# Modulation vectors moved among the mLSTM heads, the second half's operand built in pieces, and a GEMM's first weights fetched an iteration earlier

## The chip, the cores and the metric

The kernel runs on one core of one Trainium2 chip. The metric is the device time of one execution in microseconds (us). Engines are named as in the profile: PE is TensorE, which multiplies matrices; PEld its weight loads; DVE is VectorE, ACT ScalarE, POOL GpSimd, SP SyncE, which here only issues transfers (DMAs).

## The reference, cut to what matters

Two transformer blocks run one after the other on one sequence of 1024 positions with 1024 channels, all in float32. The first has three attention branches and an MLP; the second a mixer (a two-direction mLSTM with four heads beside a pooling branch) and another MLP. In the second block the normalised inputs and the updates are scaled and shifted by six modulation vectors that come from one conditioning vector `c`:

```python
def second_block(x, c, w_ada, b_ada, ...):
    c_act = jax.nn.silu(c)
    mod = c_act @ w_ada[l] + b_ada[l]          # 6 x 1024 numbers
    sh1, sc1, gt1, sh2, sc2, gt2 = jnp.split(mod, 6, axis=-1)
    h = _modulate(_rmsnorm(x, g_mix[l]), sh1, sc1)       # h * (1 + scale) + shift
    x = x + gt1[:, None, :] * _mixer(h, ...)
    h = _modulate(_rmsnorm(x, g_ffn[l]), sh2, sc2)
    a = jnp.square(jax.nn.relu(jnp.einsum('bsd,df->bsf', h, w_ff1[l])))
    x = x + gt2[:, None, :] * jnp.einsum('bsf,fd->bsd', a, w_ff2[l])
    return _rmsnorm(x, g_final)
```

Each MLP is `relu(h @ w1)**2 @ w2` with 1024 x 4096 and 4096 x 1024 weights. So `sh1` and `sc1` are wanted when the first MLP has ended and the mixer's input is normalised; the other four (`gt1`, `sh2`, `sc2`, `gt2`) not before the mixer's output.

## The kernel before, in words

Every float32 operand is split into a high and a low part of a faster format, and a product of two operands is three matmuls: high x high, low x high, high x low. For weights, `parts_of` (L1246) makes the high part `wh` by an ACT copy (L1249) and the remainder `wl` by a DVE subtraction (L1250). `product` (L1253) is a block of 128 x 512 results: four slices of the contraction, so twelve matmuls.

**One MLP** (`mlp`, L1233, called for both blocks) multiplies by a scheme with seven products for a 2 x 2 split of the matrices instead of eight. Its operand is normalised in two halves. The helper `make_t` (L1105) builds the second half's: a first piece at once, and `rest` (L1128), which forms the operands that the tables `TQ["t2"]`, `["t3"]`, `["t4"]` hold. `rest` works in four PSUM banks, four channel blocks at a time; six banks (`mm_bank`) are all that products and `rest` have. The **first GEMM** starts with products that need only the first half (`first_of`, L1313): blocks 4, 5, 6 and 0, then `rest`, then blocks 1, 2 and 3. Then 16 iterations follow (`for m in range(NM)`), each with weight sums on POOL (`sums`, L1306), five to seven products, and results written to DRAM. The **second GEMM** runs over four quarters `ch` of the hidden layer. A quarter loads blocks of the weights `a11`, `a21`, `a22`, `a12`, POOL forms their sums (`s_`, L1462, and further sums at L1483, L1484), and seven groups of products follow, each with an operand that `second` (L1393) reads back from DRAM and splits. In `ch` 0 the order is `a11`, `s_`, `a11` again (now a difference), and so on.

**The modulation vectors** come from the generator `ada` (L1152). There are twelve groups of 512 columns. For a group DVE takes eight weight tiles of 128 x 512 (`adaw`, two buffers, 256 KB a transfer on SP's queue), multiplies the first by a scalar for each partition (L1180) and adds seven more (fused multiply-add, L1182) into `ada`; PE transposes the sum in four pieces (L1189), and DVE adds them up into `mod`. `tick` after a DVE instruction takes one step of the generator, and puts what it issues behind that instruction. In the kernel before, ticks stand so close together in the first MLP that all twelve groups end in it.

**The heads.** `mlstm` (L1877) goes over eight chunks in two directions for each head. A step makes two PE products into a PSUM bank, DVE updates the state `C` (L1898) and computes the denominator `den` (L1902 to L1904), and ACT or DVE writes the head's rows. Between steps PE works on other products (`fill2`, `steps`).

What order the instructions of each engine have is fixed when the program is built, by a scheduler that follows the code's data and its issue order. Each engine runs its own list in that order, and waits for others by semaphores.

Of the kernel before, what the change touches and what calls it, by code (L numbers as in the profile page):

```python
# [60 lines left out]
def block_kernel(ctx, tc, x, mem, positions, g_mix, w_in, b_gate, sinks, g_mem, w_mem_kv, w_proj_swa, w_proj_dsa,  # L61
# [1090 lines left out]
    def ada(modp):  # L1152
# [80 lines left out]
    def mlp(PB, xt, d, w1, w2, scale, post, begin, middle, tick=lambda ins: None, gains=None, each=lambda i, e: None,  # L1233
# [66 lines left out]

        e1s, e2s, sas = {}, {}, {}
# [20 lines left out]
        rest_t.pop()()  # L1322
        begin[2]()
        first_of(1)
        first_of(2)
        first_of(3)
        e1s[0] = w_of(wep, 0, "we", 2)
        sums(0)
        for m in range(NM):
# [15 lines left out]
            tick(V.tensor_tensor(q12, p5, u2, op=OP.add))  # L1345
# [3 lines left out]
            tick(V.tensor_tensor(q12, a, q12, op=OP.add))  # L1349
# [10 lines left out]
            tick(V.tensor_tensor(q22, p5, u3, op=OP.add))  # L1360
# [26 lines left out]
        braw = hA([P, DC, 512], F32, tag="h_lo")  # L1387
        nb = [0]

        def second(n, ch):  # L1390
            i = nb[0]
            nb[0] += 1
            r = braw[:, 4 * (i % 2):4 * (i % 2) + 4]  # L1393
            nc.sync.dma_start(r, d[n][:, 4 * ch:4 * ch + 4, :])
            j = 1 if i == 27 else i % 3
            t_ = ((hA, "h_hi"), (PB, "h_hi"), (PB, "h_lo"))[j]
# [728 lines left out]
```

## Time and profile before

| what | us |
|---|---|
| median of 3 runs | 2686.01 (2683.36 to 2688.73) |
| the profiled execution | 2684.82 |
| its span in the trace | 2683.1 |
| PE busy | 2522.5 |
| DVE busy | 1905.7 |
| ACT busy | 1198.5 |
| POOL busy | 985.1 |

The span is the stretch from the first to the last instruction in the trace; the profiled execution has 1.7 us beside it. The first MLP runs from about 880 to 1600 us, the heads from 1684 to 1910, the second MLP from about 1990 to the end. "Idle before" in a row is the time in which the engine had nothing to run ahead of that instruction, with the arrow to the instruction on another engine that released it. PEclk is the granted clock of TensorE: 1.00 is 2.4 GHz and 0.50 is 1.2 GHz.

### The profile page before, as it was taken

To read this page: it belongs to the slowest core of one execution; us is meant where nothing else is said; L and a number is where in the kernel's file an instruction comes from. 1 tells how busy PE (TensorE), PEld (TensorE's weight loads), DVE (VectorE), ACT (ScalarE), POOL (GpSimd) and SP (SyncE) were. 2 spreads that over 40 slices of the span, in tenths; PEclk is the share of its full clock that TensorE was granted. 3 is DMA by queue.
4 is the path that set the end of the run, shared out by engine and by line. 5 is a ranking of instruction groups with operands and counts; after the bars stand their busy time and mean duration, and the time that the engine had idled before them with its cause. 6 is when DMAs were issued, how large, how long until landed. Compare 5 with 4: busy or idle time off the path is not lost. (4 is left out here: it accounts for less than half of the span.)

```text
span 2683.1 us, 34924 instructions
## 1 busy us (share of the span) xinstructions
PE 2522.5 (94%) x12560; PEld 2108.3 (79%) x12560; DVE 1905.7 (71%) x3208; ACT 1198.5 (45%) x2218; POOL 985.1 (37%) x727
## 2 busy tenths in 40 slices
PE   7999999999999888997999969999998999999997
PEld 6899987788878677786777856888786788778886
DVE  7685868844455667877999996655557455698898
ACT  6575764434334534444433332332435455534333
POOL 3001123431002344445565651111433444576554
PEclk9999999999999899998999989999998999999999
DMA  3121023221155366658754312322452544654431
GB/s 115 52 57 47 25 64 102 83 71 32 60 178 171 103 223 212 192 184 293 246 199 153 110 32 62 125 80 63 143 162 92 194 160 161 244 203 152 170 110 63
DMA packets 284257, 348.02 MB, mean 130 GB/s; under 512 B 14364, under 2 KB 191284, under 8 KB 276916
## 3 DMA queue, kind: packets, MB, share of 16 engines
q1 hardware_dynamic: 242404, 259.95, 30.4%
q10 hardware_dynamic: 40720, 82.70, 8.5%
q0 software_dynamic: 960, 3.15, 0.3%
q8 instruction: 99, 1.62, 0.2%
q14 instruction: 74, 0.61, 0.1%
HBM read 256.54 MB, written 89.19 MB: 129 GB/s over the span
## 5 line engine op out<-in xcount | busy, mean ns | idle before, releaser
L1255 PE MATMUL mm<-h_hi,wh 128*128 128x512 f32 (+1 forms) x1136 | 456.3, 402 | 33.6 <-DVE q L1120 10.3
L1257 PE MATMUL mm<-h_hi,wl 128*128 128x512 f32 (+1 forms) x1136 | 452.0, 399 | 22.8 <-DVE wl L1250 22.8
L1256 PE MATMUL mm<-h_lo,wh 128*128 128x512 f32 (+1 forms) x816 | 321.6, 394 | 0.0
L1255 PEld LDWEIGHTS mm<-h_hi,wh 128*128 128x128 f32 x1136 | 221.9, 195 | 82.8 <-ACT wh L1249 13.0
L1257 PEld LDWEIGHTS mm<-h_hi,wl 128*128 128x128 f32 x1136 | 221.4, 195 | 75.3 <-DVE wl L1250 29.6
L1249 ACT CAST wh<-q 128x1024 fp32r<-128x1024 f32 x116 | 122.0, 1053 | 345.3 <-PE mm L1256 294.3
L1256 PE MATMUL mm<-h_hi,wh 128*128 128x512 f32 (+1 forms) x624 | 246.1, 395 | 0.0
L1250 DVE TENSOR_TENSOR wl<-q,wh 128x1024 fp32r<-128x1024 f32 x116 | 192.2, 1659 | 22.4 <-ACT wh L1249 21.0
L1256 PEld LDWEIGHTS mm<-h_lo,wh 128*128 128x128 f32 x816 | 157.8, 193 | 31.4
L1401 POOL TENSOR_TENSOR h_hi<-h_lo,h_hi 128x512 fp32r<-128x512 f32 x76 | 126.2, 1679 | 127.8 <-ACT h_hi L1400 127.6
L133 ACT CAST wh<-wr 128x1024 fp32r<-128x1024 f32 (+5 forms) x107 | 97.2, 911 | 151.6 <-PE mm L418 47.1
L1255 PE MATMUL mm<-q,wh 128*128 128x512 f32 x384 | 150.1, 391 | 0.0
L1256 PE MATMUL mm<-q,wh 128*128 128x512 f32 x384 | 149.7, 390 | 0.0
L1257 PE MATMUL mm<-q,wl 128*128 128x512 f32 x384 | 149.6, 390 | 0.0
L1256 PEld LDWEIGHTS mm<-h_hi,wh 128*128 128x128 f32 x624 | 121.7, 195 | 24.1
L134 POOL TENSOR_TENSOR wl<-wr,wh 128x1024 fp32r<-128x1024 f32 (+5 forms) x40 | 78.3, 1964 | 160.6 <-ACT wh L133 159.1
L1641 PE MATMUL mm<-h_hi,wh 128*128 128x512 f32 x320 | 131.6, 411 | 0.9 <-DVE kn L1674 0.8
L1643 PE MATMUL mm<-h_hi,wl 128*128 128x512 f32 x320 | 126.5, 395 | 0.0
L1642 PE MATMUL mm<-h_lo,wh 128*128 128x512 f32 x320 | 125.4, 392 | 0.8 <-DVE h_lo L1081 0.8
L1250 DVE TENSOR_TENSOR wl<-we,wh 128x1024 fp32r<-128x1024 f32 x50 | 79.1, 1582 | 59.8 <-ACT wh L1249 55.9
L1255 PE MATMUL mm<-h_lo,wh 128*128 128x512 f32 (+1 forms) x304 | 115.4, 380 | 0.6 <-ACT wh L1249 0.6
L598 ACT ACTIVATE sbit<-sbit 128x1024 bf16<-128x1024 bf16 (+2 forms) x99 | 93.6, 947 | 50.0 <-DVE sbit L597 48.1
(594 smaller groups left out, 6991.2 us busy)
## 6 DMA issues: line engine op xcount, KB each, us to landing
h_lo<-ml_t SPq DMA_DIRECT2D x32, 1024.0 KB
adaw<-in_w_ada_dram SPq DMA_DIRECT2D x96, 256.0 KB
h_lo<-ml_q SPq DMA_DIRECT2D x24, 1024.0 KB
wr<-in_w_in_dram SPq DMA_DIRECT2D x42, 512.0 KB
wr<-in_w_out_dram SPq DMA_DIRECT2D x32, 512.0 KB
q<-in_w_mlp_out_dram SPq DMA_DIRECT2D x16, 1024.0 KB
q<-in_w_ff_dram SPq DMA_DIRECT2D x16, 1024.0 KB
ml_t<-h_lo ACTq DMA_DIRECT2D x60, 256.0 KB
```

What stands on the lines that cost most here:

```text
L133: A.copy(hi, r)
L134: (eng or V).tensor_tensor(lo, r, raw(hi), op=OP.subtract)
L598: A.activation(b, b, AF.Copy, accum_out=cnt[:, j:j + 1])
L1249: A.copy(hi, r)
L1250: (eng or V).tensor_tensor(lo, r, raw(hi), op=OP.subtract)
L1255: mm(a, wt[0][:, k], b[0][:, k, sl], start=(k == 0), stop=False)
L1256: mm(a, wt[0][:, k], b[1][:, k, sl], start=False, stop=False)
L1257: mm(a, wt[1][:, k], b[0][:, k, sl], start=False, stop=(k == 3))
L1401: (G if c % 2 else V).tensor_tensor(lo[:, c], r[:, c], raw(hi[:, c]), op=OP.subtract)
L1641: mm(a, hi[:, k, :], r_hi, start=(k == 0), stop=False)
L1642: mm(a, hi[:, k, :], r_lo, start=False, stop=False)
L1643: mm(a, lo[:, k, :], r_hi, start=False, stop=(k == DC - 1))
```

## The change

Three edits, of which the second and third act in both MLPs.

1. Ticks in the first MLP become fewer (in the first GEMM three in two iterations instead of eight, in the second a few in each quarter). Four groups of columns, `sh1` and `sc1`, have to be done there, which `while done[0] < 4` makes sure of; a fifth has its DVE instructions there. The others go on in the heads: a tick stands after each step's first `den` operation, and in the forward direction after every second row update. What would be left is finished behind the last head, where the second normalisation's gain (`gain_of(1, ...)`) is computed. The pool with the `adaw` buffers stays open until then.
2. `rest` becomes a generator. It takes two banks for two channel blocks, forms `t2` and `t4` in them, and hands over; between its pieces stand the first products of blocks 1, 2 and 3.
3. In the last iteration of the first GEMM the operand of the second one's first group (`second("q12", 0)`, now `b_1`) and its first weights (`w_1`) are fetched. The weights come as two pieces of 256 columns into tiles `we` and `wr` of the first GEMM, and are split into parts right behind the loop. The whole block `a11` is still loaded for POOL's sums.

```diff
         def rest():
-            b = [mm_bank() for _ in range(4)]
             t2, t3, t4 = (TQ[n] for n in ("t2", "t3", "t4"))
-            for c in range(4):
-                norm(4 + c, b[c])
-            for c in range(4):
-                V.tensor_tensor(src(c), b[c], src(c), op=OP.subtract)
-                A.copy(src(4 + c), b[c])
-                V.tensor_tensor(b[c], b[c], t1[c], op=OP.subtract)
-                split_to(t2[0][:, c, :], t2[1][:, c, :], b[c])
+            for cs in ((0, 1), (2, 3)):
+                b = {c: mm_bank() for c in cs}
+                for c in cs:
+                    norm(4 + c, b[c])
+                for c in cs:
+                    V.tensor_tensor(src(c), b[c], src(c), op=OP.subtract)
+                    A.copy(src(4 + c), b[c])
+                    V.tensor_tensor(b[c], b[c], t1[c], op=OP.subtract)
+                    split_to(t2[0][:, c, :], t2[1][:, c, :], b[c])
+                for c in cs:
+                    z = first(4 + c, t1[c])
+                    V.tensor_tensor(b[c], z, b[c], op=OP.subtract)
+                    split_to(t4[0][:, c, :], t4[1][:, c, :], b[c])
+                yield
             for c in range(4):
                 split_to(hi1[:, 4 + c, :], lo1[:, 4 + c, :], src(4 + c))
+            yield
             for c in range(4):
                 split_to(t3[0][:, c, :], t3[1][:, c, :], src(c))
-            for c in range(4):
-                z = first(4 + c, t1[c])
-                V.tensor_tensor(b[c], z, b[c], op=OP.subtract)
-                split_to(t4[0][:, c, :], t4[1][:, c, :], b[c])
+            yield
...
         first_of(0)
-        rest_t.pop()()
+        more = rest_t.pop()()
+        next(more)
+        first_of(1)
+        next(more)
+        first_of(2)
+        next(more)
+        first_of(3)
+        next(more)
         begin[2]()
-        first_of(1)
-        first_of(2)
-        first_of(3)
...
         for m in range(NM):
             u2, q11, u3, q12 = s1s[m % 4], q11s[m % 4], u3s[m % 2], q12s[m % 2]
+            if m == NM - 1:
+                b_1 = second("q12", 0)
+                w_1 = []
+                for u in range(2):
+                    w_1.append(wep([P, 4, 256], F32, tag="we", bufs=2) if u else wp([P, 4, 256], F32, tag="wr", bufs=2))
+                    nc.sync.dma_start(w_1[u], quarter_of(0, 0, 0, u * 256, 256))
...
-            tick(V.tensor_tensor(q12, p5, u2, op=OP.add))
+            r = V.tensor_tensor(q12, p5, u2, op=OP.add)
+            if m % 2:
+                tick(r)
...
         save_later()
+        w_1 = [parts_of(r) for r in w_1]
         wep.close()
...
-            if not late_ and e % 4 != 1 and (hf or e < 4):
+            if not late_ and e == 2 and not (hf and ch_[0] == 3):
                 tick(r)
...
-            b = second("q12", ch)
+            b = second("q12", ch) if ch else b_1
...
-            for e, wt in blocks(a11):
+            for e, wt in blocks(a11, None if ch else w_1):
...
         if hf == 0:
-            for _ in ada_:
-                pass
...
+            while done[0] < 4:
+                next(ada_)
+            gain_of(0, "g_mix_2")
...
                 den = wk_([P, 1], tag="den", bufs=3)
-                V.tensor_scalar(den, nm[:, P:P + 1], -1.0, flo[:, r0 + c:r0 + c + 1], op0=OP.mult, op1=OP.max)
+                tick1(V.tensor_scalar(den, nm[:, P:P + 1], -1.0, flo[:, r0 + c:r0 + c + 1], op0=OP.mult, op1=OP.max))
...
-                    V.scalar_tensor_tensor(hm(c), nm[:, :P], den, hm(c), op0=OP.mult, op1=OP.add)
+                    r = V.scalar_tensor_tensor(hm(c), nm[:, :P], den, hm(c), op0=OP.mult, op1=OP.add)
+                    if i % 2:
+                        tick1(r)
...
     pool_out(3)
+    for _ in ada_:
+        pass
+    gain_of(1, "g_ffn_2")
```

The first place is DVE's list at the start of the first MLP, where `rest` and the first products meet. L1295 (L1301 after) evicts a first product, L1110 to L1144 (to L1141 after) and L1120 belong to `rest`, `wl` at L1250 (L1256) is a weight remainder. Before:

```order
L1120 TENSOR_TENSOR h_lo_1869_9100<-h_lo_1737_8334,h_hi_1868_9099 128x512 x2
L1120 TENSOR_TENSOR q_1875_9114<-mm_1911_9314,q_1874_9113 128x512
L1120 TENSOR_TENSOR q_1877_9116<-h_lo_1737_8334,q_1876_9115 128x512 x4
L1144 TENSOR_TENSOR mm_1908_9311<-t512_1894_9213,mm_1908_9311 128x512
L1144 TENSOR_TENSOR mm_1909_9312<-t512_1895_9215,mm_1909_9312 128x512
L1144 TENSOR_TENSOR mm_1910_9313<-t512_1896_9217,mm_1910_9313 128x512
L1120 TENSOR_TENSOR q_1879_9118<-mm_1908_9311,q_1878_9117 128x512
L1120 TENSOR_TENSOR q_1879_9118<-mm_1909_9312,q_1878_9117 128x512
L1120 TENSOR_TENSOR q_1879_9118<-mm_1910_9313,q_1878_9117 128x512
L1144 TENSOR_TENSOR mm_1911_9314<-t512_1897_9219,mm_1911_9314 128x512
L1295 TENSOR_TENSOR h_hi_1736_8333<-mm_1916_9392,h_hi_1736_8333 128x512
```

After:

```order
L1137 TENSOR_TENSOR mm_1908_9311<-mm_1908_9311,t512_1894_9213 128x512
L1137 TENSOR_TENSOR mm_1909_9312<-mm_1909_9312,t512_1895_9215 128x512
L1110 SCALAR_TENSOR_TENSOR mm_1916_9370<-h_lo_1737_8334,cols_4_75,tp_1893_9208 128x512
L1120 TENSOR_TENSOR q_1875_9114<-mm_1908_9311,q_1874_9113 128x512
L1120 TENSOR_TENSOR q_1875_9114<-mm_1909_9312,q_1874_9113 128x512
L1141 TENSOR_TENSOR mm_1908_9311<-t512_1894_9213,mm_1908_9311 128x512
L1141 TENSOR_TENSOR mm_1909_9312<-t512_1895_9215,mm_1909_9312 128x512
L1301 TENSOR_TENSOR h_hi_1736_8333<-mm_1914_9353,h_hi_1736_8333 128x512
L1120 TENSOR_TENSOR q_1879_9118<-mm_1908_9311,q_1878_9117 128x512
L1120 TENSOR_TENSOR q_1879_9118<-mm_1909_9312,q_1878_9117 128x512
L1135 TENSOR_TENSOR h_lo_1737_8334<-mm_1915_9369,h_lo_1737_8334 128x512
```

Before, the eviction in the last row comes when `rest` is all but done; after, one stands in the midst of it, and `t4` (`q_1879`) of the first two blocks is formed ahead of the later two blocks' `t2`.

The second place is DVE's list in the first GEMM of the first MLP, over about one iteration. `ada<-adaw` is the modulation. Before:

```order
L1349 TENSOR_TENSOR h_lo_1737_8334<-mm_1999_9911,h_lo_1737_8334 128x512
L1182 SCALAR_TENSOR_TENSOR ada_1980_9799<-adaw_1989_9854,silu_1832_8844,ada_1980_9799 128x512
L1359 TENSOR_TENSOR h_lo_1737_8334<-mm_2005_9943,h_hi_1736_8333 128x512
L1360 TENSOR_TENSOR h_lo_1737_8334<-mm_1993_9868,h_lo_1737_8334 128x512
L1182 SCALAR_TENSOR_TENSOR ada_1980_9799<-adaw_1996_9905,silu_1832_8844,ada_1980_9799 128x512
L1250 TENSOR_TENSOR wl_2017_10033<-we_1994_9881,wh_2016_10032 128x1024
L1365 TENSOR_TENSOR h_lo_1737_8334<-mm_2007_9964,h_lo_1737_8334 128x512
L1182 SCALAR_TENSOR_TENSOR ada_1980_9799<-adaw_2000_9926,silu_1832_8844,ada_1980_9799 128x512
```

After:

```order
L1400 TENSOR_TENSOR h_lo_1737_8334<-mm_2011_10027,h_hi_1736_8333 128x512
L1401 TENSOR_TENSOR h_lo_1737_8334<-mm_2001_9958,h_lo_1737_8334 128x512
L1256 TENSOR_TENSOR wl_2022_10114<-we_2002_9971,wh_2021_10113 128x1024
L1406 TENSOR_TENSOR h_lo_1737_8334<-mm_2012_10045,h_lo_1737_8334 128x512
L1186 SCALAR_TENSOR_TENSOR ada_1946_9592<-adaw_1987_9876,silu_1832_8844,ada_1946_9592 128x512
L1256 TENSOR_TENSOR wl_2025_10136<-wr_2009_10020,wh_2024_10135 128x512
L1410 TENSOR_TENSOR h_lo_1737_8334<-mm_2014_10063,h_hi_1736_8333 128x512
L1411 TENSOR_TENSOR h_lo_1737_8334<-mm_2014_10063,h_lo_1737_8334 128x512
```

Of three modulation instructions in such a stretch one is left.

The third place is DVE's list at the beginning of head 0. Before:

```order
L1903 TENSOR_TENSOR den_2741_14854<-den_2741_14854,sc_2738_14848 128x1
L1898 SCALAR_TENSOR_TENSOR C_2745_14878<-C_2740_14852,dec_2723_14764,sc_2744_14876 128x129
L1904 RECIPROCAL den_2741_14854<-den_2741_14854 128x1
L1902 TENSOR_SCALAR den_2746_14880<-tp_2743_14873,flo_2721_14754 128x1
L1898 SCALAR_TENSOR_TENSOR C_2751_14902<-C_2745_14878,dec_2723_14764,tp_2750_14900 128x129
L1903 TENSOR_TENSOR den_2746_14880<-den_2746_14880,tp_2743_14873 128x1
L134 TENSOR_TENSOR wl_2787_15071<-wr_2788_15072,wh_2786_15070 128x1024
L1904 RECIPROCAL den_2746_14880<-den_2746_14880 128x1
```

After:

```order
L1929 TENSOR_SCALAR den_2688_14690<-sc_2685_14683,flo_2654_14529 128x1
L1186 SCALAR_TENSOR_TENSOR ada_2681_14664<-adaw_2523_13796,silu_1832_8844,ada_2681_14664 128x512
L1930 TENSOR_TENSOR den_2688_14690<-den_2688_14690,sc_2685_14683 128x1
L1925 SCALAR_TENSOR_TENSOR C_2692_14712<-C_2687_14688,dec_2656_14539,sc_2691_14710 128x129
L1931 RECIPROCAL den_2688_14690<-den_2688_14690 128x1
L1929 TENSOR_SCALAR den_2693_14714<-tp_2690_14707,flo_2654_14529 128x1
L1925 SCALAR_TENSOR_TENSOR C_2698_14738<-C_2692_14712,dec_2656_14539,tp_2697_14736 128x129
L1930 TENSOR_TENSOR den_2693_14714<-den_2693_14714,tp_2690_14707 128x1
L134 TENSOR_TENSOR wl_2733_14889<-wr_2734_14890,wh_2732_14888 128x1024
L1186 SCALAR_TENSOR_TENSOR ada_2681_14664<-adaw_2682_14666,silu_1832_8844,ada_2681_14664 128x512
```

Two multiply-adds now stand among the `den` and `C` instructions of two steps here; in all of head 0 there are thirteen, and two of the tensor-by-scalar form.

## Rows read from the trace of the kernel before

**Rows 1.** The page's head and part 1: busy us of each engine

```profile
span 2683.1 us, 34924 instructions
...
PE 2522.5 (94%) x12560; PEld 2108.3 (79%) x12560; DVE 1905.7 (71%) x3208; ACT 1198.5 (45%) x2218; POOL 985.1 (37%) x727
```

**Rows 2.** TensorE's waits: line, releaser; us in total, times, longest us

```profile
PE tp L1189 <- DVE ada L1182: 25.5, 7, 8.8
PE mm L1257 <- DVE wl L1250: 23.1, 12, 9.7
PE tp L1024 <- DVE q L1009: 20.3, 4, 15.9
PE mm L1255 <- ACT wh L1249: 10.7, 7, 3.8
PE mm L1255 <- DVE q L1120: 10.3, 2, 5.7
...
PE mm L1255 <- ACT x L1292: 6.8, 1, 6.8
...
PE mm L1255 <- ACT h_hi L1292: 6.3, 1, 6.3
```

**Rows 3.** Timeline, TensorE's three first waits for ada: start, us, engine, line

```profile
972.75 1.09 PE L1189 MATMUL tp<-ident,ada 128*128 128x128 f32 x4 [8.77 <-DVE ada L1182]
...
1017.34 0.63 PE L1189 MATMUL tp<-ident,ada 128*128 128x128 f32 x4 [3.48 <-DVE ada L1182]
...
1141.07 0.63 PE L1189 MATMUL tp<-ident,ada 128*128 128x128 f32 x4 [3.55 <-DVE ada L1182]
```

**Rows 4.** The modulation's DVE instructions: duration ns min/median/max, first and last start

```profile
L1182 DVE SCALAR_TENSOR_TENSOR ada<-adaw,silu,ada x84: 731/970/2569, 945.7 to 1444.1; 128x512 f32<-128x512 f32 x84
L1180 DVE TENSOR_SCALAR ada<-adaw,silu x12: 475/478/1402, 943.6 to 1413.0; 128x512 f32<-128x512 f32 x12
```

**Rows 5.** Windows: length, busy PE PEld DVE ACT POOL, granted clock, DMA share, GB/s

```profile
967.61:977.85 10.24, 5.10 (x14) 4.23 (x15) 6.55 (x7) 3.42 (x6) 6.04 (x4) 0.50 0.63 189
1141.69:1145.10 3.41, 3.41 (x10) 2.65 (x9) 2.72 (x3) 2.94 (x5) 1.61 (x2) 0.50 0.55 179
912.99:930.06 17.07, 9.14 (x20) 6.25 (x21) 13.75 (x20) 6.03 (x12) 2.66 (x2) 0.50 0.18 51
2032.56:2049.63 17.07, 8.77 (x19) 5.97 (x20) 14.13 (x20) 7.59 (x13) 1.57 (x1) 0.50 0.24 75
1237.26:1244.09 6.83, 6.18 (x14) 4.40 (x15) 5.82 (x9) 5.96 (x11) 3.80 (x5) 0.50 1.05 410
1257.74:1267.98 10.24, 5.23 (x12) 4.18 (x13) 7.78 (x4) 1.53 (x2) 7.89 (x5) 0.50 0.25 94
1400.00:1450.00 50.00, 45.12 (x196) 36.84 (x195) 50.00 (x58) 15.71 (x23) 25.21 (x13) 0.97 0.57 199
1684.00:1717.00 33.00, 31.59 (x192) 26.57 (x193) 26.51 (x93) 12.14 (x33) 7.03 (x6) 1.00 0.46 148
1717.00:1910.00 193.00, 192.54 (x1010) 161.82 (x1008) 112.00 (x305) 58.31 (x129) 30.20 (x59) 1.00 0.19 58
```

**Rows 6.** Timeline, TensorE's waits at the start of either second GEMM

```profile
1237.87 0.80 PE L1255 MATMUL mm<-h_hi,wh 128*128 128x512 f32 x1 [3.85 <-ACT wh L1249]
...
1262.75 0.80 PE L1257 MATMUL mm<-h_hi,wl 128*128 128x512 f32 x1 [9.71 <-DVE wl L1250]
...
2338.84 0.50 PE L1257 MATMUL mm<-h_hi,wl 128*128 128x512 f32 x1 [2.13 <-DVE wl L1250]
...
2361.97 0.79 PE L1257 MATMUL mm<-h_hi,wl 128*128 128x512 f32 x1 [4.92 <-DVE wl L1250]
```

**Rows 7.** Timeline there in the first MLP: DVE remainders, POOL sums

```profile
1252.28 12.68 DVE L1250 TENSOR_TENSOR wl<-q,wh 128x1024 fp32r<-128x1024 f32 x3 [8.61 <-ACT wh L1249]
...
1251.11 4.68 POOL L1483 TENSOR_TENSOR q<-q,q 128x1024 f32<-128x1024 f32 x2
```

**Rows 8.** Timeline, DVE in a step of a later head

```profile
1799.71 0.22 DVE L1902 TENSOR_SCALAR den<-sc,flo 128x1 f32<-128x1 f32 x1 [2.65 <-PE sc L1890]
```

More of the change, by code (lines that the diff above doesn't have):

```diff
@@ L1191, in ada @@
             V.tensor_tensor(m4, m4, bada[:, g * 4:(g + 1) * 4], op=OP.add)
+            done[0] = g + 1
+    done = [0]
     modp = Pool("modp", side="right")
@@ L1299, in first_two, with second, quarter_of @@
                 nc.scalar.dma_start(d["away"][:, m - 4, 1, :], q11)
+        nb = [0]
+        braw = []
+        def second(n, ch):
+            i = nb[0]
+            nb[0] += 1
+            if not braw:
+                braw.append(hA([P, DC, 512], F32, tag="h_lo"))
+            r = braw[0][:, 4 * (i % 2):4 * (i % 2) + 4]
+            nc.sync.dma_start(r, d[n][:, 4 * ch:4 * ch + 4, :])
+            j = 1 if i == 27 else i % 3
+            t_ = ((hA, "h_hi"), (PB, "h_hi"), (PB, "h_lo"))[j]
+            t_ = t_[0]([P, DC, 512], F32R, tag=t_[1])
+            hi, lo = t_[:, 0:4], t_[:, 4:8]
+            for c in range(4):
+                A.copy(hi[:, c], r[:, c])
+                (G if c % 2 else V).tensor_tensor(lo[:, c], r[:, c], raw(hi[:, c]), op=OP.subtract)
+            return hi, lo
+        def quarter_of(ch, j, i, c0, n):
+            return w2[ch * 1024:(ch + 1) * 1024, :].rearrange("(u two p) e -> two p u e", two=2, p=P)[j][
+                :, :, i * 512 + c0:i * 512 + c0 + n]
         e1s, e2s, sas = {}, {}, {}
@@ L1348, in mlp @@
             product(a, half(ub, 1), B22)
-            tick(V.tensor_tensor(q12, a, q12, op=OP.add))
+            V.tensor_tensor(q12, a, q12, op=OP.add)
             relu2(q12)
@@ L1359, in mlp @@
             V.tensor_tensor(u3, a, u2, op=OP.add)
-            tick(V.tensor_tensor(q22, p5, u3, op=OP.add))
+            V.tensor_tensor(q22, p5, u3, op=OP.add)
             relu2(q22)
@@ L1385, in x_back @@
                 nc.sync.dma_start(xt[hf][:, e0:e0 + 4, :], d["x"][:, e0:e0 + 4, halves(hf)])
[L1387 to L1396, printed above, removed]
-            t_ = t_[0]([P, DC, 512], F32R, tag=t_[1])
-            hi, lo = t_[:, 0:4], t_[:, 4:8]
-            for c in range(4):
-                A.copy(hi[:, c], r[:, c])
-                (G if c % 2 else V).tensor_tensor(lo[:, c], r[:, c], raw(hi[:, c]), op=OP.subtract)
-            return hi, lo
         def upd(hf, e, a, sl=slice(0, 512)):
@@ L1427, in upd_s, with blocks @@
             return upd(hf, e, a)
-        def blocks(r, eng=None):
+        def blocks(r, done=None):
             for u in range(2):
-                wt = parts_of(r[:, :, u * 256:(u + 1) * 256], eng)
+                wt = done[u] if done else parts_of(r[:, :, u * 256:(u + 1) * 256])
                 for e in range(2):
@@ L1565, in block_kernel, with gain_of @@
     V.tensor_tensor(gsq, cols[:, r0:r0 + 8], cols[:, r0:r0 + 8], op=OP.mult)
+    def gain_of(i, n):
+        r0, _ = ROWS[n]
+        sc = mod[:, 8 + 24 * i:16 + 24 * i]
+        V.scalar_tensor_tensor(gsc[:, 8 * i:8 * i + 8], sc, 1.0, cols[:, r0:r0 + 8], op0=OP.add, op1=OP.mult)
     def post_mlp1(hf, st):
         if hf == 0:
-            for _ in ada_:
-                pass
-            for i, n in ((0, "g_mix_2"), (1, "g_ffn_2")):
-                r0, _ = ROWS[n]
-                sc = mod[:, 8 + 24 * i:16 + 24 * i]
-                V.scalar_tensor_tensor(gsc[:, 8 * i:8 * i + 8], sc, 1.0, cols[:, r0:r0 + 8], op0=OP.add, op1=OP.mult)
+            while done[0] < 4:
+                next(ada_)
+            gain_of(0, "g_mix_2")
             r0, _ = ROWS["g_final"]
@@ L2015, in block_kernel @@
     hBp.close()
+    modp.close()
     ypl = Pool("ypl")
```

10 lines of the change are left out of this document (5 added, 5 removed).

## The prediction

> **What bounds the kernel now.** I read the page's first part, then the waits of the TensorE queue, then windows and timelines of the stretches that those waits name. The profiled execution took 2684.8 us, 1.7 more than its span and 1.2 under the median of 2686.0, so a gain counted on its trace carries over to the median. TensorE is busy for 2522.5 of 2683.1 us [rows 1]; only the other 160.6 us, and the stretches in which its clock is at the lower of its two levels, can be won. The reader should see in [rows 2] that a few places hold most of the waits the change can reach: the transposes of the modulation vectors (25.5 us in 7 waits), the weight remainders `wl` at the start of the second GEMM (23.1, both MLPs), the first product after the normalised operand (6.8 and 6.3 behind ACT, 10.3 behind DVE, one pair for each MLP), and one 15.9 us wait at the first MLP's end. After the longer waits the granted clock is 0.50, so 1.2 GHz instead of 2.4, and whatever TensorE does there costs double [rows 5].
>
> **Part 1, modulation vectors: what leaves the first MLP.** Twelve groups of one tensor-by-scalar and seven fused multiply-adds run there [rows 4]; five groups stay, and seven, so 56 DVE instructions and their 256 KB loads, move into the four heads. Four transposes stay of twelve, and the order puts many more matmuls between a group's last multiply-add and its transpose. All seven waits, three of which are 8.77, 3.48 and 3.55 us [rows 3], had the transpose nearly level with the DVE instruction it needs. I let 2 of the 25.5 us remain: +23.5. Clock: the 10.24 us at 0.50 behind the first wait hold 5.10 us of work, which at full clock is 2.55; the row of 3.41 us behind another wait would give 1.7, and two more waits have such a row: at most 7.6, taken 5.5 since other stalls lie near. Part 1 gives **+29.0** in the first MLP; bounds +15 (only the waits in the first GEMM go) and +33.
>
> **Part 1, what the heads pay.** No trace shows a multiply-add among the heads' steps. From the rest of the profile: a step's `den` chain leaves DVE idle 2.65 us between steps [rows 8], and over heads 1 to 3 DVE is busy 112.0 of 193.0 us. Some 41 of the 56 instructions go there: 36 x 0.97 + 5 x 0.48 = 37 us [rows 4] into 81 idle ones; I charge 1 us. Head 0 has no such room: DVE is busy 26.5 of 33.0 us, TensorE 31.6 [rows 5]. Its share, 13 x 0.97 + 2 x 0.48 = 13.6, makes 40.1 us of DVE work in 33.0: 7 us over, and TensorE's order there is fixed, so it waits. Taken **-8.0**. One end is 0, if DVE's later slack takes the overhang; the other has each of the 56 on the path, 49 x 0.97 + 7 x 0.48 = 51 us.
>
> Whether these instructions run at the minimum or the maximum of their row depends on what lies beside them: 731 ns at best, 970 in the median, 2569 at worst [rows 4], and the first MLP has POOL busy for about half of the time in the window shown against 30.2 of 193.0 us in the heads. The Trainium skill (GPSIMD Engine Reference, Specifications) says that GpSimd's SBUF interfaces are shared with VectorE and that DVE instructions with two SBUF inputs contend there; the multiply-add has two, so by that rule the heads would see the minimum. At 0.73 us head 0's overhang would be 13 x 0.73 + 2 x 0.48 + 26.5 - 33.0 = 4 us, and the time 3 us lower. I keep the median.
>
> **Part 2, the second half's operand traced between the first products.** Before, `rest` takes four of six PSUM banks for its whole length, so the first products stop for banks: waits of 6.3 and 5.7 us in the first MLP and 6.8 and 4.6 in the second [rows 2], with 9.14 and 8.77 us of work at half clock around them [rows 5]. If all of that went, 12.0 + 4.6 and 11.4 + 4.4, together 32 us, would be won. But the pieces issue the same DVE and ACT work, and DVE is busy 13.8 of the 17.1 us [rows 5]; the evictions of the first products now stand between the pieces and free their banks sooner, while the later pieces come later. By the order about three matmuls more are done when full work resumes some 2 to 4 us sooner. I take +3 for each MLP, **+6.0**; bounds -1 (the late pieces hold up the main loop) and +16 for each.
>
> **Part 3, the second GEMM's first weights and operand fetched in the first GEMM's last iteration.** In the first MLP the wait of 3.85 us [rows 6] is for weights whose transfer was issued too late; with them there it goes, with 6.18/2 = 3.1 us of clock [rows 5]. That puts TensorE about 7 us nearer to the next wait, 9.71 us [rows 6], which is for the summed block `s_`: its POOL sums (2.3 us an instruction, one after another) and its DVE remainders, 12.68 us for three [rows 7]. That chain starts from a transfer of the same queue; since the fetches ahead of it are now earlier and two modulation loads fewer stand among them, I let it move by 7 us too, so the second wait neither grows nor shrinks: **+7.0**, bounds 0 (all 7 reappear in the second wait) and +19 (both waits and their half clock go). In the second MLP the first wait is 2.13 and the second 4.92 [rows 6]; there I let 2.1 go, add back 0.6: **+1.5**, bounds -2 and +7.
>
> **End of the first MLP.** Its 15.9 us wait [rows 2] is behind DVE sums of squares. A few multiply-adds now stand in its last chunk that were done before, each 0.97 us [rows 4], and one weight remainder comes later: **-2.0**, bounds -5 and +2.
>
> Sum: 29.0 - 8.0 + 6.0 + 7.0 + 1.5 - 2.0 = 33.5. From the profiled 2684.8 that is 2651.3; on the median's footing 2686.0 - 33.5 = 2652.5.
>
> **Rivals.** (a) *The heads' steps become DVE-bound.* Place: between the first and second `den` operation. The multiply-add sits in front of a `den` operation, and head output, state update and the next TensorE step queue behind it; if TensorE's fixed order has no cover, all 51 us are paid instead of 8: 2652.5 + 43 = 2695.5. It decides from 41.5/56 = 0.74 us of delay for each moved instruction. For it: head 0's 40.1 in 33.0. Against: heads 1 to 3 have 81 idle us, and TensorE is busy 192.5 of 193.0 with filling products between steps. What would add to it is the clock: in these 33.0 us it is 1.00 although TensorE idles 1.4 us [rows 5], and after an 8.77 us wait it was 0.50 [rows 3, 5]. The Trainium skill (TensorE: Matmul & The Clock Gate, HAM oscillation) warns that waits recurring between short bursts throttle TensorE again each time; were all of head 0 throttled, its 31.6 us would take up to 31.6 more. By that sentence alone the sum would come out at 2684, no change; the trace has no such stretch among the heads.
>
> (b) *The starts are hidden wholly.* The 32 us of part 2 go instead of 6: 2652.5 - 26 = 2626. For it: all four waits name the operand's chain or a bank. Against: DVE's 13.8 of 17.1.
>
> (c) *Gains given back inside the MLP.* In the second GEMM's window shown DVE is busy 50.0 of 50.0 us [rows 5], so the 9.7 us of waits there (25.5 less the 15.8 of [rows 3]) may only become waits on other DVE results, with their clock: 9.7 + 3.4 less, 2665.5. Against: the multiply-adds themselves are much of that 50.0. Akin: the prefetch only moves the stall to `s_`, 8.5 less and 3 more at the MLP's end: 2664.
>
> **How the numbers follow.** Forecast 0.52; (c) and its kin 0.22; (b) 0.10; (a) 0.09; 0.07 for several terms near their bad ends, 0.05 of it within 0.2% (5.4 us, about what a measurement can tell from no change). So faster 0.86, same 0.05, slower 0.09. The likeliest case's own range is 2640 to 2664. The range reaches past (b) only in part and short of (a): 2630 to 2680.
>
> **What would show it.** The waits of transposes on `ada` fall from 25.5 to under 5 us in the first MLP; the first MLP's first wait shrinks and its sum of 12 falls by about 3 only; the 3.85 us wait is gone and the one for `s_` stays near 10; in head 0 DVE is busy throughout and TensorE waits for `den` or C some 7 us more, at clock 1.00; heads 1 to 3 are as long as before within 2 us. The prediction is wrong if the heads together grow by over 20 us, if the starts give over 10 us each, or if DVE's waits in the second GEMM take up what the transposes left.

## The result: 0.9% faster, by less than the prediction's middle

The changed kernel takes 2661.7 us in the median of 4 runs (2655.2 to 2666.7), the kernel before 2685.4 beside it: a ratio of 0.991, 95% interval 0.9889 to 0.9931. The gain is 24 us. The prediction's range was 2630 to 2680 and its forecast faster, by 33.5 us; 10 us are missing.

The page's head of the changed kernel, and its part 1 (busy us of each engine), which answer to [rows 1]:

```profile
span 2665.0 us, 34925 instructions
...
PE 2516.8 (94%) x12560; PEld 2103.1 (79%) x12560; DVE 1888.1 (71%) x3208; ACT 1198.3 (45%) x2218; POOL 977.4 (37%) x727
```

TensorE's waits, the five that answer to [rows 2] (line, releaser; us in total, times, longest us):

```profile
PE mm L1261 <- ACT wh L1255: 32.6, 13, 6.7
PE tp L1024 <- DVE q L1009: 22.4, 4, 17.7
PE mm L1263 <- DVE wl L1256: 18.4, 11, 8.0
...
PE mm L1261 <- DVE h_hi L1301: 3.3, 2, 2.3
...
PE tp L1193 <- DVE ada L1186: 2.5, 1, 2.5
```

The reader should see that the transposes' waits are down from 25.5 to 2.5 us, that the only one left is not in the first MLP (below), that the waits on remainders went from 23.1 to 18.4, but that waits for `wh` rose from 10.7 to 32.6, and the wait at the MLP's end (L1024) from 20.3 to 22.4. Much of that rise is the same stall under another name: two of the waits for `wh`, 4.29 and 6.74 us, stand at the MLPs' starts, where the waits behind the operand (6.8, 6.3 and 10.3 us in [rows 2]) are down to 3.3.

Where the time went is best read from TensorE's lead. Both programs issue the same matmuls in nearly the same order apart from the 48 of the modulation, so the n-th of the others was looked up in both traces, and its start in the one taken from its start in the other. The profiled executions compared are 2684.8 and 2666.7 us; the second is the slowest of its four, 5 us above their median, so the leads below add up to 18 us and not to 24. Lead at the end of each stretch, in us:

| stretch | lead at its end | gained in it | predicted |
|---|---|---|---|
| until the first MLP | 1.5 | | |
| first MLP, its start | 6.6 | +5.1 | +3 |
| first MLP, the first GEMM's loop | 21.2 | +14.7 | with the next but one +29 |
| transition to the second GEMM | 24.3 | +3.1 | +7 |
| first MLP, rest of the second GEMM | 40.0 | +15.7 | see above |
| end of the first MLP | 40.0 | 0.0 | -2 |
| the four heads | 13.4 | -26.6 | -8 |
| second MLP, its start | 19.4 | +6.1 | +3 |
| second MLP, transition | 19.3 | 0.0 | +1.5 |
| end | 18.4 | -1.0 | |

So the first MLP did what was expected of it, and the heads took most of that back. Some of both is TensorE's own work: the transposes are left out of the count, and a group of four holds the queue for about 0.35 us wherever it stands, so eight groups that now run among the heads are 2.8 of the 26.6 us and of the first MLP's 30.4. The timeline of TensorE in the changed kernel (start, us, engine, line; the wait before and its releaser in brackets), at the first MLP's start, at its transition, at its end, in head 0, and at the second MLP's start:

```profile
910.73 0.50 PE L1261 MATMUL mm<-h_hi,wh 128*128 128x512 f32 x1 [1.06 <-DVE h_hi L1301]
...
918.11 0.50 PE L1261 MATMUL mm<-q,wh 128*128 128x512 f32 x1 [2.25 <-DVE h_hi L1301]
...
923.19 0.79 PE L1261 MATMUL mm<-h_hi,wh 128*128 128x512 f32 x1 [4.29 <-ACT wh L1255]
...
1229.93 0.79 PE L1261 MATMUL mm<-h_hi,wh 128*128 128x512 f32 x1 [6.69 <-ACT wh L1255]
...
1239.13 0.80 PE L1263 MATMUL mm<-h_hi,wl 128*128 128x512 f32 x1 [7.98 <-DVE wl L1256]
...
1536.18 0.66 PE L1024 MATMUL tp<-ident,q 128*128 128x128 f32 x2 [17.70 <-DVE q L1009]
...
1662.68 0.46 PE L1920 MATMUL sc<-v,kn 128*128 128x129 f32 x2 [1.73 <-DVE h_hi L1935]
...
1666.51 0.90 PE L1193 MATMUL tp<-ident,ada 128*128 128x128 f32 x3 [2.50 <-DVE ada L1186]
...
1677.37 0.55 PE L1893 MATMUL sc<-qT,tmp 128*128 128x128 f32 x1 [3.42 <-DVE h_lo L1935]
...
2029.41 0.80 PE L1261 MATMUL mm<-h_hi,wh 128*128 128x512 f32 x1 [6.74 <-ACT wh L1255]
```

At the start three waits of 7.6 us in all stand for 12 before [rows 2]. At the transition the 3.85 and 9.71 us of [rows 6] became 6.69 and 7.98, so their sum rose. In head 0 three waits are new, all on DVE. Windows of the changed kernel over the heads (columns as in [rows 5]), the last two being stretches of low clock:

```profile
1640.00:1684.00 44.00, 34.99 (x181) 29.55 (x180) 34.90 (x95) 13.45 (x31) 9.98 (x6) 0.84 0.61 200
1684.00:1760.00 76.00, 73.28 (x385) 61.80 (x385) 52.33 (x144) 19.46 (x48) 10.15 (x9) 0.98 0.46 144
1760.00:1898.00 138.00, 133.87 (x687) 110.28 (x685) 94.57 (x237) 41.70 (x92) 22.18 (x53) 1.00 0.29 87
1666.16:1672.99 6.83, 5.83 (x23) 5.15 (x24) 5.67 (x22) 1.21 (x6) 0.00 (x0) 0.50 0.75 230
1676.40:1683.23 6.83, 5.86 (x18) 5.02 (x19) 6.83 (x12) 1.58 (x4) 4.23 (x2) 0.50 0.25 77
```

In the 44 us around head 0 TensorE idles 9.0 us, and twice its clock falls to 0.50 behind these waits, with 5.8 and 5.9 us of work in the two stretches, about half of it lost time. In the other heads another 6.9 us are idle in 214. The `ada` instructions of this stretch (duration ns min/median/max, first and last start):

```profile
L1186 DVE SCALAR_TENSOR_TENSOR ada<-adaw,silu,ada x49: 732/744/1099, 1648.8 to 1831.9; 128x512 f32<-128x512 f32 x49
L1184 DVE TENSOR_SCALAR ada<-adaw,silu x7: 475/480/486, 1647.3 to 1811.8; 128x512 f32<-128x512 f32 x7
```

DVE's timeline in head 0:

```profile
1661.04 1.23 DVE L1879 TENSOR_TENSOR E<-E,an 128x1024 f32<-128x1024 f32 x1 [1.67 <-DMA E<-row]
1662.18 0.35 DVE L1935 SCALAR_TENSOR_TENSOR h_hi<-sc,den,h_hi 128x128 f32<-128x128 f32 x1
1664.57 1.10 DVE L1186 SCALAR_TENSOR_TENSOR ada<-adaw,silu,ada 128x512 f32<-128x512 f32 x1 [2.04 <-DMA adaw<-in_w_ada_dram]
1665.59 0.20 DVE L1929 TENSOR_SCALAR den<-tp,flo 128x1 f32<-128x1 f32 x1
1665.72 0.74 DVE L1186 SCALAR_TENSOR_TENSOR ada<-adaw,silu,ada 128x512 f32<-128x512 f32 x1
1666.38 0.14 DVE L1930 TENSOR_TENSOR den<-den,tp 128x1 f32<-128x1 f32 x1
```

A head's row update (L1935) that TensorE waits for stands behind `E`, which waited 1.67 us for its transfer; the next `den` stands behind a multiply-add that waited 2.04 us for its weights, and behind the multiply-add itself, 1.10 us. Each of these instructions stands in DVE's queue and starts only behind the one in front.

### The profile page after: what moved, and what is told of

Read it like the earlier page. It is cut to its first block, busy times and chain, and to the rows that moved or that the text cites. A ratio compares the mean times of both kernels' runs of the same rounds, so it can differ in the third digit from the quotient of the medians.

```text
span 2665.0 us, 34925 instructions
## 1 busy us (share of the span) xinstructions
PE 2516.8 (94%) x12560; PEld 2103.1 (79%) x12560; DVE 1888.1 (71%) x3208; ACT 1198.3 (45%) x2218; POOL 977.4 (37%) x727
## 5 line engine op out<-in xcount | busy, mean ns | idle before, releaser
L1261 PE MATMUL mm<-h_hi,wh 128*128 128x512 f32 (+1 forms) x1136 | 450.3, 396 | 33.5 <-ACT wh L1255 31.9
L1263 PE MATMUL mm<-h_hi,wl 128*128 128x512 f32 (+1 forms) x1136 | 447.3, 394 | 18.6 <-DVE wl L1256 18.4
L1262 PE MATMUL mm<-h_hi,wh 128*128 128x512 f32 (+1 forms) x624 | 243.8, 391 | 0.0
L1256 DVE TENSOR_TENSOR wl<-q,wh 128x1024 fp32r<-128x1024 f32 x112 | 184.3, 1650 | 19.4 <-ACT wh L1255 18.1
L1262 PEld LDWEIGHTS mm<-h_lo,wh 128*128 128x128 f32 x816 | 155.8, 191 | 30.4
L1256 DVE TENSOR_TENSOR wl<-we,wh 128x1024 fp32r<-128x1024 f32 x52 | 83.7, 1610 | 65.2 <-ACT wh L1255 64.2
L1323 DVE TENSOR_TENSOR h_hi<-h_lo,h_hi 128x512 fp32r<-128x512 f32 x76 | 117.9, 1576 | 3.6 <-ACT h_hi L1322 3.6
```

The source lines that it names most:

```text
L1256: (eng or V).tensor_tensor(lo, r, raw(hi), op=OP.subtract)
L1261: mm(a, wt[0][:, k], b[0][:, k, sl], start=(k == 0), stop=False)
L1262: mm(a, wt[0][:, k], b[1][:, k, sl], start=False, stop=False)
L1263: mm(a, wt[1][:, k], b[0][:, k, sl], start=False, stop=(k == 3))
L1323: (G if c % 2 else V).tensor_tensor(lo[:, c], r[:, c], raw(hi[:, c]), op=OP.subtract)
```

## Experiments

All ratios are to the kernel before in the same set of runs, medians with the 95% interval; 0.001 is 2.7 us. The theories: the heads' loss is (A) DVE waiting at the head of its queue for loads with two buffers, or (B) DVE's own time, where a step leaves it none; the rival of the whole is that the heads are longer for another reason.

**1. No modulation in the heads.**

```diff
+        V.memset(mod, 1.0)
...
-            if i < 12 * DC:
+            if i < 5 * DC:
...
-        for g in range(12):
+        for g in range(5):
```

> The changed kernel without groups 6 to 12 of the modulation: their 56 DVE instructions and loads are left out, so the heads carry none of them (four transposes of the fifth group stay), and the two gates and the second shift and scale are left at one. If the heads' added work is the whole of what is missing from the gain (the trace shows TensorE's 40 us lead before head 0 fall to 13.4 behind head 3, 26.6 us), this runs in about 2661.7 - 26 = 2636 us, with the heads as long as before within 3 us. Rival: the heads are longer for another reason (the order of other instructions there changed); then over 2650.

Measured: 2634.4 us, 0.9824 (0.9809 to 0.9838). The lead is 41.7 us ahead of head 0 and 42.0 behind head 3. So the whole loss is the moved work; by the ratios it is 0.991 - 0.9824, 23 us in the median, where the two profiles gave 26.6. This trace also tells where DVE has room: between two `den` of a backward pass's later steps it is idle some 2.7 us of 3.4 in heads 1 and 2. At the first step of a pass, at the fifth of a forward pass, and nearly throughout head 0, it is idle for 0.6 us a step or less.

**2. The same instructions without their loads.**

```diff
         def load(i):
-            if i < 12 * DC:
+            if 5 * DC + 2 <= i < 12 * DC:
+                ld.append(fix[i % 2])
+            elif i < 12 * DC:
                 w = modp([P, 512], tag="adaw", bufs=2)
...
                 ld.append(w)
+                fix[i % 2] = w
```

> The changed kernel in which all modulation groups behind the fifth multiply by the last two weight tiles loaded, so the same 56 DVE instructions stand in the heads without 54 of their 256 KB loads; the vectors from them are wrong. Theory A (DVE stands at the head of its queue waiting for a load, two buffers being too few for ticks this close, and all den and C work queues behind it): most of the 26.6 us goes, 2640 to 2647. Theory B (the DVE time itself, 13.6 us more in head 0's 33, is what is late): little goes, 2655 to 2662.

Measured: 2649.9 us, 0.9881 (0.9865 to 0.9898), between the two theories. The heads lose 15.8 us of lead instead of 26.6: about 11 go with the loads (8 by the ratios, whose intervals leave 1 to 15), and the larger part stays without them. That part is the DVE instructions and the transposes; the run does not tell the two apart.

**3. Four weight buffers in the heads.**

```diff
-                w = modp([P, 512], tag="adaw", bufs=2)
+                w = (deep[0] if deep and i % 4 > 1 else modp)([P, 512], tag="adaw", bufs=2)
...
-                load(g * DC + k + 2)
+                while len(ld) < (4 if deep else 2) and nx[0] < 12 * DC:
+                    load()
```

> The changed kernel with four weight buffers instead of two for the modulation once the heads begin (two more from the heads' own pool), loads issued four ahead. Theory A (waits for loads): 2643 to 2650, and no idle time of DVE in front of a modulation instruction. Theory B (DVE time): 2656 to 2662. If loads lose to the heads' other transfers on the queue, no better than 2661.

Measured: 2656.2 us, 0.9905 (0.989 to 0.992), not to be told from the changed kernel. DVE has no idle time left in front of a modulation instruction, as A said, and the heads lose 20.7 us of lead against 26.6 in the one profile of each; the ratios do not show that. So B's range came true: A's waits are worth 1 us by the ratios, and at most 8 by their intervals. Without any loads the heads are 5 us better still (20.7 against 15.8). Part of that is in DVE's waits for the heads' own transfers, `E` and `qa`, over the heads; the rows are of the changed kernel, of this one, and of run 2:

```profile
DVE E L1879 <- DMA E<-row: 6.2, 4, 2.3
...
DVE E L1886 <- DMA E<-row: 3.9, 3, 1.4
DVE qa L1907 <- DMA qa<-row: 1.4, 1, 1.4
...
DVE E L1883 <- DMA E<-row: 2.3, 2, 1.2
```

In the kernel before these waits are 1.8 us. They stay with four buffers and go with the loads, so the loads delay other transfers too, though ACT's queue issues those of `E` and SP's the loads.

**4. Nothing in head 0, denser in the others.**

```diff
-                tick1(V.tensor_scalar(den, ...))
+                (tick1 if hd else (lambda r: None))(V.tensor_scalar(den, ...))
...
-                    if i % 2:
+                    if hd:
                         tick1(r)
```

> The changed kernel with no tick in head 0 and, in heads 1 to 3, a tick behind every den and every row update (24 a head instead of 20). Head 0 lost 16.3 us of TensorE's lead and the other three 10.3, by the trace. If a modulation instruction costs only where DVE is full (head 0), this gives back 14 to 16 us: 2645 to 2648. Rival: each moved instruction costs about the same wherever it stands (26.6/56 = 0.47 us), because it delays its own step's chain: 2660 or slower.

Measured: 2653.6 us, 0.9894 (0.9879 to 0.9909). Head 0 loses nothing (lead 44.2 before and 43.7 behind it), but heads 1 to 3 now lose 19, where they lost 10. Half of that, 9.7 us, is lost at the border of heads 1 and 2, around a wait of TensorE for `C` and 3.4 us at half clock:

```profile
1746.63 0.64 PE L1917 MATMUL tp<-C,qa 128*128 128x129 f32 x2 [4.78 <-DVE C L1923]
```

Ahead of that `C` DVE had waited 1.83 us for `E`'s transfer and 1.38 for a weight tile. So "only head 0 is full" does not hold. Nor is there one price for an instruction: 56 in heads 1 to 3 cost 19 us here, and 40 cost 6.3 in run 9.

**5 to 7. Each part alone.** The edits are those of the change.

> The kernel before with the modulation's move alone. By the trace of the changed kernel it wins 30 us in the first MLP and loses 26 in the heads: 2680 to 2684, a gain of 0.1%. By the prediction's own terms (29 - 2 won, 8 lost): 2666.

Measured: 2670.7 us, 0.9957 (0.9944 to 0.9971). A gain of 11.5 us; so the expectation from the trace, 2680 to 2684, failed, and the prediction's terms, 2666, came nearer. Its own trace has the heads lose 24.4 us of lead (36.9 to 12.5) with neither of the other parts, so their loss is part 1's; the stretch up to the heads wins more than the 30 counted on, 35.6.

> The kernel before with the second half's operand traced in pieces alone. By the trace the two starts give 5.1 and 6.1 us: 2674 us. By the prediction: 6 us, 2679. If the ticks of the first MLP, still dense here, take back what the first start gives, 2679 too.

Measured: 2671.0 us, 0.9958 (0.9944 to 0.9973). 11 us as the trace had it, with the dense ticks of before in place; the prediction's 6 was too little.

> The kernel before with the second GEMM's first weights and operand fetched an iteration earlier, alone. By the trace the transitions give 3.1 us and nothing: 2682, hardly to be told from no change. By the prediction 8.5: 2677. If the wait only moves to the summed block, 2685.

Measured: 2682.1 us, 0.9999 (0.999 to 1.0009). Nothing. Its trace at the first MLP's transition, TensorE:

```profile
1248.96 0.80 PE L1255 MATMUL mm<-h_hi,wh 128*128 128x512 f32 x1 [7.13 <-ACT wh L1249]
...
1258.17 0.80 PE L1257 MATMUL mm<-h_hi,wl 128*128 128x512 f32 x1 [7.99 <-DVE wl L1250]
```

and POOL's, where the block's sum begins:

```profile
1242.09 1.09 POOL L1280 DMA_DIRECT2D ml_t<-h_lo  x2
...
1243.19 4.64 POOL L1474 TENSOR_TENSOR q<-q,q 128x1024 f32<-128x1024 f32 x2
```

The prefetched weights do their block without a wait, and TensorE stands 7.13 us before the next one, and 7.99 before its second half: 15.1 us, for 13.6 before. POOL's sum starts as soon as POOL has issued the last iteration's stores; no transfer holds it up. The three parts add up: 11.5 + 11.3 + 0.3 = 23.1 of 24.

**8. All groups in the first MLP, transposes later.** Parts 2 and 3, the ticks of before, and two more yields before a group's transposes.

```diff
                 yield
             yield
+            yield
+            yield
             m4 = mod[:, g * 4:(g + 1) * 4]
```

> Parts 2 and 3 with the ticks of the kernel before, so all twelve groups stay in the first MLP, but with three ticks instead of one between a group's last multiply-add and its transposes. If the transposes waited only because they stood level with that multiply-add, most of the 30 us that the first MLP won is won without the heads' 26.6: 2640 to 2648, faster than the changed kernel. Rival: DVE is the bound of the second GEMM (50 of 50 us busy) and its waits move to other results: 2660 or more.

Measured: 2675.3 us, 0.9968 (0.9957 to 0.9979): the expectation failed, and no better than part 2 alone. TensorE's waits in it:

```profile
PE mm L1265 <- DVE wl L1258: 27.3, 15, 8.0
PE tp L1195 <- DVE ada L1186: 23.8, 4, 7.3
```

Four transposes, all in or at the end of the first GEMM, still wait 3.6 to 7.3 us, though three ticks stand ahead of them; why was not found. In the second GEMM none waits any more, but remainders do, 0.7 to 2.5 us at a time behind the transition. There the rival was right: DVE is full, and the wait goes to the next thing that DVE makes.

**9 to 11. Where DVE has room.** Two ticks (three in the last) behind each update of the first block's output projection, ahead of the first MLP; the rest in heads 1 to 3, behind every `den` (9) or at chosen steps (10, 11). A group's transposes come two ticks (three in the last) behind its last multiply-add while the output projection runs. The expectations call the three early2, placed2 and placed3.

```diff
                 V.tensor_tensor(d, a, d, op=OP.add)
+                if hf or e > 2:
+                    for _ in range(2):
+                        tick1(r)
...
-            yield
+            for _ in range(lag[0]):
+                yield
...
+    TICKS = {(1, 1): (0, 1, 2, 2, 2, 2, 2, 1), (1, 0): (0, 0, 1, 1, 0, 1, 1, 0), ...}
...
                 r = V.reciprocal(den, den)
+                for _ in range(TICKS.get((hd, d_), (0,) * NT)[i]):
+                    tick1(r)
```

> The changed kernel with two ticks behind each update of the first block's output projection (13 units, DVE about half busy there), so seven groups are done by the end of the first MLP; the other five run in heads 1 to 3 with a tick behind every den. Theory B (a moved instruction costs where DVE is full): the output projection has room and costs 0 to 2 us; 40 instructions in heads 1 to 3 at 0.25 to 0.34 us each cost 10 to 14 instead of 23: 2648 to 2653. Rival (the cost is in the number of transposes and loads, wherever they stand): as slow as the changed kernel, 2660.

Measured: 2645.4 us, 0.9859 (0.9844 to 0.9873). That is under the range: the heads lose 6.3 us of lead, less than the 10 to 14 expected, and the output projection 3.9, more than 0 to 2. Windows there (columns as in [rows 5]), of the kernel before and of this one:

```profile
770.00:890.00 120.00, 119.03 (x558) 97.14 (x558) 61.30 (x75) 49.54 (x72) 25.77 (x19) 1.00 0.60 188
...
770.00:890.00 120.00, 116.98 (x550) 94.54 (x549) 81.88 (x97) 48.34 (x69) 30.16 (x18) 1.00 0.71 226
```

DVE is busy for 81.9 of 120 us instead of 61.3, and TensorE idle for 3 instead of 1. Two groups' transposes take 0.9 us there as well, so 2.9 of the 3.9 us are found: 2 of waits, the longest 1.14 us for a remainder from DVE, and the transposes' own time.

> As early2, but the five groups' ticks stand only behind the den work of those steps of heads 1 to 3 in which the trace without modulation in the heads leaves DVE idle for 1 to 2.6 us (two ticks in a step with 2.1 us or more, none at a step whose DVE time is full). Theory B: they cost 0 to 4 us together: 2637 to 2644, within 8 us of the kernel with none of them (2634.4). Rival (each delays its own step's chain): as early2, 2650.

Measured: 2645.1 us, 0.9856 (0.9841 to 0.9871). The heads lose 3.4, as expected; the output projection and what stands around it lose 4.5, more than expected, so the time is 1 us outside what B said. It is not to be told from run 9's, where the ticks stand behind every `den`: that choosing the steps helps is read from the leads, 3.4 against 6.3, in one profile of each.

> As placed2 with three ticks for each unit of the output projection, so eight groups are done by the end of the first MLP and four are left for the heads. A unit there has about 2.8 us of DVE idle, and three multiply-adds take 2.2 to 2.9: if that still fits, 2635 to 2642; if not, each of 13 units loses some tenths and the time is 3 to 6 us above placed2.

Measured: 2646.0 us, 0.9861 (0.9844 to 0.9877). The heads lose 1.5, the output projection 7.9: three do not fit. DVE waits 22.3 us for loads in the whole kernel, in 20 waits, and two of TensorE's waits in the projection, 2.2 us together, are for transfers of the input.

**12. The transition's differences on DVE.** On top of placed2; in `ch` 0 the differences also come behind the third block of products instead of the first:

```diff
-                if e == 0:
+                if e == (0 if ch else 2):
...
-                        G.tensor_tensor(a21[:, q_], a11[:, q_], a21[:, q_], op=OP.subtract)
-                        G.tensor_tensor(a11[:, q_], s_[:, q_], a11[:, q_], op=OP.subtract)
+                        (G if ch else V).tensor_tensor(a21[:, q_], a11[:, q_], a21[:, q_], op=OP.subtract)
+                        (G if ch else V).tensor_tensor(a11[:, q_], s_[:, q_], a11[:, q_], op=OP.subtract)
```

> placed2, and in the first quarter of each second GEMM the four differences that POOL computes beside the summed block's weight remainders are computed by DVE, which is idle for 9 us there. In the trace three remainders take 11.4 us beside those POOL instructions, one takes 1.2 alone, and TensorE waits 8.0 and 4.8 us for them. If POOL's work beside them is what slows the remainders, they take about 1.2 us each, the second wait of either transition goes, and the time is 2633 to 2640 (placed2: 2645). If the block is late because its sum on POOL (4.7 us) and its transfer are, or because DVE now does the differences first, the waits stay: 2643 to 2648.

Measured: 2633.9 us, 0.9824 (0.9807 to 0.984), the fastest of all, by the ratios 23 us under the changed kernel and 8.6 under placed2. The first MLP's transition in the changed kernel, DVE's timeline:

```profile
1229.91 9.17 DVE L1256 TENSOR_TENSOR wl<-q,wh 128x1024 fp32r<-128x1024 f32 x1 [9.12 <-ACT wh L1255]
...
1239.01 2.35 DVE L1256 TENSOR_TENSOR wl<-q,wh 128x1024 fp32r<-128x1024 f32 x2
```

POOL's there:

```profile
1224.16 4.64 POOL L1488 TENSOR_TENSOR q<-q,q 128x1024 f32<-128x1024 f32 x2
1228.75 4.66 POOL L1509 TENSOR_TENSOR q<-q,q 128x1024 f32<-128x1024 f32 x2
1233.37 4.63 POOL L1510 TENSOR_TENSOR q<-q,q 128x1024 f32<-128x1024 f32 x2
```

The expectation's "three remainders take 11.4 us" ran them together. The first takes 9.17 us, the other two 1.2 each. The first starts beside POOL's differences (from 1228.75 on) and ends 1.08 us after the last of them, which ends at 1238.00; the other two run when POOL has stopped. The same place with the differences on DVE, DVE's timeline:

```profile
1230.93 3.35 DVE L1515 TENSOR_TENSOR q<-q,q 128x1024 f32<-128x1024 f32 x1 [5.72 <-POOL q L1494]
...
1235.34 2.35 DVE L1262 TENSOR_TENSOR wl<-q,wh 128x1024 fp32r<-128x1024 f32 x2
1237.61 2.35 DVE L1516 TENSOR_TENSOR q<-q,q 128x1024 f32<-128x1024 f32 x2
```

and TensorE's:

```profile
1234.32 0.80 PE L1267 MATMUL mm<-h_hi,wh 128*128 128x512 f32 x1 [7.57 <-ACT wh L1261]
...
1236.60 0.80 PE L1269 MATMUL mm<-h_hi,wl 128*128 128x512 f32 x1 [1.06 <-DVE wl L1262]
```

With POOL idle two remainders take 2.35 us. DVE's first difference still meets the second half of POOL's sum, which ends at 1233.19: it takes 3.35 us and again ends 1.09 us behind it. The wait for the first half stays, 7.57 us, since the copy to `wh` waits for POOL's sum; the second falls from 7.98 to 1.06. In the second MLP the waits fall less, from 1.98, 1.10 and 5.07 (placed2) to 1.28 and 4.37, so "the second wait of either transition goes" came true in one. The lead gained at the two transitions goes from 3.6 to 9.3 us and from -0.2 to 3.9 (placed2 and this kernel), 9.7 us together. The Trainium skill (GPSIMD Engine Reference, Specifications) names a cause that fits, SBUF interfaces which GpSimd shares with VectorE, with contention where a VectorE instruction has two SBUF inputs. The trace agrees: both these DVE instructions have two, and each stood until POOL was done. The runs show that POOL's work beside it is what counts, not through which port.

## Why the prediction was right, and which term was mis-sized

The direction and the range held, and so did much of the mechanism: part 1's gain in the first MLP (+29.0 predicted; 30.4 in the lead, of which 2.8 are the transposes' own time), the end of that MLP (-2 and 0), and a loss in the heads that is the moved work's. That the total came within 10 us is in part luck. The heads' term missed by 15 us and part 3 by 8.5, one way; part 2 missed by 5 and two smaller terms by 3, the other way. By the prediction's own sign, heads that grow by over 20 us, it is wrong about the heads.

*The heads' term, -8.0, is the one that was off: it measured -23* (run 1 against the changed kernel), inside the bounds 0 to -51. Two steps of it failed. "I charge 1 us" for heads 1 to 3 rested on an average, 37 us of work into 81 idle ones. About half of the idle time lies in the later steps of the backward passes (run 1), and the ticks stood at every step, the full ones too: 10 us of lead went there, and 19 when they were denser (run 4). And head 0's "7 us over" took DVE's time alone; it lost 16.3. The terms left at nothing are the clock, which fell twice, the loads (8 to 11 us over all heads by run 2, by run 3 in part because two buffers are too few, in part through the loads' traffic), and the transposes of seven groups, some 2.5 us. The multiply-adds themselves were cheaper than charged: 744 ns at the median in the heads against 970.

Rival (a) was thus a good part of what happened, at 0.4 us on average for each of 56 instructions and not the 0.74 from which it would have decided. The sentence of the Trainium skill beside it (TensorE: Matmul & The Clock Gate, HAM oscillation) said that short bursts with waits between them throttle TensorE; the trace agrees in part: the clock fell in head 0, where it had been 1.00, but for two stretches of 6.8 us and not for all of it.

*Part 2, +6.0, measured 11.3* (interval 7 to 15), between the forecast and rival (b)'s 32. The argument that DVE is the bound was right for the size of what is left (waits of 7.6 and 6.7 us), but the half-clock stretches shrank with the waits, from 17.07 us [rows 5] to the 10.24 of these windows of the changed kernel, and that was not in the 3 us. DVE is busy for 9.9 and 10.2 us of each:

```profile
918.64:928.88 10.24, 5.47 (x12) 3.65 (x12) 9.93 (x16) 4.50 (x8) 0.82 (x1) 0.50 0.18 51
2024.56:2034.80 10.24, 5.29 (x12) 3.66 (x13) 10.23 (x16) 6.29 (x11) 1.77 (x2) 0.50 0.18 62
```

*Part 3, +8.5, measured 0* (run 7). The step that failed is "I let it move by 7 us too": the chain of the summed block did not move with the fetches. In the first MLP it does not start "from a transfer of the same queue" either. POOL's sum, its first link, starts right behind POOL's last work for the first GEMM, at 1246.4 us before (4.7 ahead of POOL's row in [rows 7]) and at 1243.2 with part 3 alone, where TensorE is 3.1 us ahead from before the transition: no sooner, then. From there POOL runs the sum and four differences without a gap, and the remainder that TensorE waits for ends 1.1 us behind the last of them (run 12), so the 7 us came back as a longer wait. In the second MLP the sum does wait for its transfer, 2.90 us with part 3 alone, and starts at 2339.5 us as it did before (2339.6). That was the lower bound, "all 7 reappear in the second wait", and the kin of rival (c).

Rival (c) itself, gains given back in the second GEMM, did not come true for the change, whose second GEMM won 15.7 us; run 8 shows that it does where the modulation stays there.

What stays open: some 1 us of the 3.9 that the output projection loses with two ticks a unit, why transposes still wait with three ticks ahead of them (run 8), and how the loads delay the heads' other transfers.

## What to carry to other kernels

Count an engine's idle time step by step at the places where the new work will stand, not as a sum over a stage: 41 instructions among 81 idle us still cost 10 us of lead, and 40 at steps chosen for their room cost 3.4. Count a moved load's traffic too, for deeper buffers took DVE's waits for the loads away and left most of the cost. A prefetch ahead of a chain on two other engines moves the wait and not its end; look first for what the chain's engines do to each other (here POOL beside DVE).

## What the runs showed of the hardware

A DVE subtraction of two SBUF operands of 128x1024 takes 1.2 us alone. Of the 269 weight remainders of that size in the changed kernel's trace 74 took longer than 1.25 us, up to 12.2, and each of these ended 1.08 or 1.09 us behind the end of a POOL `tensor_tensor`. DVE did not share the time with POOL, it stood: at 1229.91 through the rest of four POOL instructions that ran without a gap, and the next remainder, with POOL idle, took 1.2. Moving POOL's differences away from two such places was worth 8.6 us by the ratios (their intervals leave 2 to 15) and 9.7 us of lead.

TensorE's clock fell to 1.2 GHz after waits as short as 1.7 and 2.5 us close together in head 0, and in head 1 after waits of 0.89 and 0.74 us with short products between them. These windows are the 6.7 us that hold the latter two waits, and what follows them (columns as in [rows 5]):

```profile
1738.00:1744.67 6.67, 5.04 (x40) 4.52 (x39) 5.43 (x15) 1.24 (x2) 1.20 (x2) 1.00 0.44 136
1744.67:1748.08 3.41, 3.41 (x14) 3.02 (x13) 2.56 (x6) 1.06 (x4) 3.33 (x2) 0.50 0.39 132
```

A wait of 3.48 us in the kernel before, ahead of 1017.34 us [rows 3], left the clock at 1.00 for the 12.66 us behind it:

```profile
1017.34:1030.00 12.66, 12.66 (x58) 10.58 (x59) 8.44 (x11) 4.99 (x8) 7.94 (x5) 1.00 0.62 201
```
